# Modulation by quarters: one megabyte holds two feature tiles by 1024 columns, added up in SBUF

## The chip, the core and the metric

One core of a Trainium2 chip runs the whole program once per execution. The metric is the device time of one execution in microseconds. A trace of one profiled execution shows every instruction on the engines: PE (matrix multiply, with its weight loads listed apart as PEld), DVE (vector), ACT (scalar), POOL (GpSimd) and SP, whose queue issues most of the loads.

## The reference

Four transformer layers work on 256 tokens of 1024 features: two layers of a first block (which also carry a context stream of 256 tokens), then a layer with grouped attention and one with a pooling mixer, called the second block here. Each layer first turns a condition vector into six vectors of 1024 (shift, scale and gate, for the mixer and for the feed-forward part):

```python
m = jax.nn.silu(cond) @ w_ada + b_ada                    # 1024 -> 6 * 1024
h = rms_norm(x, gain) * (1 + scale) + shift
x = x + gate * mixer(h);   x = x + gate2 * conv_ffn(...)
```

In the second block the mixer's and the feed-forward part's results are normalised once more before they are added to x. The weights of one modulation are 1024 by 6144 in f32, 24 MB a layer, 96 MB for the four layers. Only two columns (the condition of the tokens and that of the context) are multiplied with them, so each byte is used in one short matmul.

## The kernel before, in words

**Work on PE.** All activations stand feature by token in SBUF. A weight matrix is loaded in pieces of up to 1 MB as two halves `w` (two buffers in all), split by ACT (line 238, `wh`) and DVE (line 240, `wl`) into two parts, and used in three matmuls a tile (`mms`, lines 285, 286, 289). Every third piece puts its split parts into the pool `x8`: seven buffers of 1 MB that also hold `y`, `sx`, `kv`, `qT`, `band` and other whole tensors; some pieces are loaded there whole.

**Modulation units.** A layer's modulation is cut into 24 units; four units make one of the six vectors. `mod_load` (line 362) loads a unit's megabyte, all eight feature tiles by 256 columns, in one piece into `x8` (20 units: those of the opening and the first twelve of layer 1) or as two halves `mw` with three buffers (76 units). `mod_unit` (line 378) issues eight short matmuls (line 387, the trace has two records for each) that leave four partial sums in four groups of 32 partitions, has ACT copy them to SBUF (line 390), calls the load of the following unit, and after a planned wait transposes both halves on PE (line 396), adds the four partial sums up in DVE (line 398) and adds the bias (line 400). `mod_units` makes a list of steps: with `ahead=1` step q loads unit q and computes unit q-1.

**Order.** PE and SP run in the order in which the program is written out, the other engines' orders are made by a planner. Two small programs fix the written order. `spread` mixes the modulation steps evenly into a list of main steps. `Line` holds generators: each yields a cost and a wait, its next part is due after both, and due parts are put in before the next step starts. So a short wait moves a part ahead of steps that follow.

**Second block.** `attention2` projects six chunks, runs eight softmax units (`unit`: scores, line 1178; transposes, line 635; values, line 1198) with twelve modulation units of the last layer (3, 0 to 11) between them, then the output matrix (`wo`), whose results give running sums for the norm (`post_sums`; squares, line 437). Then `post` runs: `post_norm` first sums the squares over features on PE (`rstd`, lines 449, 450), makes the factor `ry` (to line 468), takes two more sums on PE (line 1076), makes `m` (lines 1078 to 1081), a second factor, and the eight `ht` tiles (line 493) that the next matmuls need. `post` mixes four more modulation units in: (3, 12 to 15) after attention, (3, 16 to 19) after the feed-forward part, (3, 20 to 23) after the pooling mixer, where the two sums are ready already (line 1282). The list `late` holds these twelve units. `pool_consts` loads two `band` tiles through `w` after the first post.

The written order of the first post:

```python
def post(self, units, *args):
    self.go(self.post_norm(*args), "p")
    self.run(units)
    self.line.ensure("p")
```

Of the kernel before, what the change touches and what calls it, by code (L numbers as in the profile page):

```python
# [19 lines left out]
P = 128  # L20
D = 1024
NT = 256
# [83 lines left out]
class Stack:  # L106
    def __init__(self, ctx, tc, a, offs, out, upto=None):
# [17 lines left out]
        self.h, self.wm = {}, {}  # L125
# [189 lines left out]
    def setup(self):  # L315
# [16 lines left out]
        self.cpad = [cp.tile([P, KD, 32], F32, name=f"cpad{n}") for n in range(2)]  # L332
        for n in range(2):
            nc.vector.memset(self.cpad[n], 0.0)
            nc.scalar.activation(self.cpad[n][:, :, 0:2], cv[:, n], AF.Silu)
# [26 lines left out]
    def mod_load(self, i, n, x8=True):  # L362
        src = self.a[f"wmod{i}"][n * P * CH:(n + 1) * P * CH].rearrange("(p n) -> p n", p=P)
        if x8:
            w = self.x8("wm")
            self.nc.sync.dma_start(out=w, in_=src)
            w = w.rearrange("p (e k c) -> p e k c", e=2, k=4)
            self.wm[i, n] = [w[:, e] for e in range(2)]
            return
        self.wm[i, n] = [self.mod_half(i, n, e) for e in range(2)]  # L370

    def mod_half(self, i, n, e):
        w = self.mp.tile([P, 4, NT], F32, tag="mw", name="mw", bufs=3)
        src = self.a[f"wmod{i}"][n * P * CH:(n + 1) * P * CH].rearrange("(p n) -> p n", p=P)
        self.nc.sync.dma_start(out=w, in_=src[:, 1024 * e:1024 * e + 1024].rearrange("p (k c) -> p k c", k=4))
        return w

    def mod_unit(self, i, n, then=None):
# [3 lines left out]
        cpad = self.cpad[i // 2]  # L382
        acc = self.psum("acc", [P, 512])[:, :256]
        w = self.wm.pop((i, n))
# [18 lines left out]
    def mod_units(self, i, ns, x8=False, ahead=1):  # L403

        ns = [n if i is None else (i, n) for n in ns]

        def step(q):
            load = (lambda: self.mod_load(*ns[q], x8)) if q < len(ns) else (lambda: None)
            if q >= ahead:
                yield from self.mod_unit(*ns[q - ahead], load)  # L410
# [549 lines left out]
    def ffn(self, i, T, streams, after):  # L960
# [70 lines left out]
        for q in streams:  # L1031
            for ft in range(KD):
                self.go(down(len(groups) - 1, ft, slice(256 * q, 256 * q + 256)))
            after(q, nst[q], y)
# [30 lines left out]
    def post_norm(self, i, y, st, j, g):  # L1065
# [3 lines left out]
        yield 0, 1.2  # L1069
        ry = self.rstd(st)  # L1070
        yield 0.9, 1.5
# [81 lines left out]
    def attention2(self):  # L1153
# [59 lines left out]
        f = self.more_units((3, 0, 12))  # L1213
        seq = kx + vx + q[0] + q[1] + need("c0", "c1", "c2") + f[:2]
        seq += spread(un[0], f[2:5]) + q[2] + need("c3") + spread(un[1], f[5:7]) + q[3] + need("c4")
        seq += spread(un[2], f[7:10]) + need("c5") + spread(un[3], f[10:])
# [17 lines left out]
        for cc in range(4):  # L1234
            for f2 in range(2):
                self.go(wo(cc, f2))
        return y, nst
# [13 lines left out]
    def pool_mixer(self):  # L1251
# [34 lines left out]
        for n in (0, 1, -1, -2, 2, -3, -4, 3, -5, -6, -7, -8):  # L1286
            self.go(z(n) if n >= 0 else out(-n - 1), f"z{n}")
        line.ensure(*(f"z{-n - 1}" for n in range(KD)))
# [288 lines left out]
```

## Time and profile before

| | us |
|---|---|
| Median of 3 runs (lowest, highest) | 1829.44 (1826.78, 1840.67) |
| The profiled execution's own time | 1839.73 |
| Its span, first to last instruction | 1837.9 |
| PE busy | 1650.7 (90%) |
| DVE busy | 1180.2 (64%) |
| ACT busy | 900.9 (49%) |
| POOL busy | 133.0 (7%) |
| Moved by DMA | 288.39 MB, mean 157 GB/s |

The profiled execution's time is the span and 1.8 us around it. Busy shares are averages over stages with different limits; a stage's own rows say which wait ends last there.

### The profile page before, as it was taken

Reading aid. Unit: us, or ns where it says so; the run is one execution under the profiler, and the core shown is the slowest. Engines: PE = TensorE matmul, PEld = TensorE weight load, DVE = VectorE, ACT = ScalarE, POOL = GpSimd, SP = SyncE. Lnnn points to the kernel's source line nnn. Section 1 sums busy time; section 2 is a strip of 40 time slices with the busy share of each in tenths; the row PEclk is TensorE's granted clock in tenths of the full one; section 3 lists DMA queues with packets and bytes.
Section 4 is the critical chain, followed back from the end, with each engine's and each line's share of the span. In section 5 each row is a group of like instructions: output and inputs, shape, how many; then the busy total and the mean of one; then the engine's idle time right before and its main releaser. Section 6 shows DMA issues by size and latency. Waiting matters only on the chain.

```text
span 1837.9 us, 32872 instructions
## 1 busy us (share of the span) xinstructions
PE 1650.7 (90%) x12736; PEld 1443.7 (79%) x12736; DVE 1180.2 (64%) x2992; ACT 900.9 (49%) x2213; POOL 133.0 (7%) x162
## 2 busy tenths in 40 slices
PE   6999797999999998897799999969779999769997
PEld 5877457989889898874488888856659998459997
DVE  5665786656554567865688576746556567666665
ACT  5445554534333334554456464534446565546563
POOL 1000001000000000000001011000221012221010
PEclk9999898999999999997989999989969999789998
DMA  7334330433334332355627767465455544345552
GB/s 310 102 138 152 108 123 24 138 136 117 114 117 138 115 117 70 121 201 184 220 96 280 247 220 246 132 218 172 131 191 173 186 167 155 124 152 188 178 193 84
DMA packets 74892, 288.39 MB, mean 157 GB/s; under 512 B 8560, under 2 KB 9840, under 8 KB 69104
## 3 DMA queue, kind: packets, MB, share of 16 engines
q1 hardware_dynamic: 73152, 283.91, 45.3%
q10 hardware_dynamic: 1584, 2.38, 0.4%
q8 instruction: 100, 1.64, 0.4%
q14 instruction: 56, 0.46, 0.1%
HBM read 285.21 MB, written 1.05 MB: 156 GB/s over the span
## 4 chain that ended last, share of the span: by engine, by line
PE 65%; DVE 13%; DMA 13%; ACT 6%; issue 2%; POOL 1%; SPq 0%; ACTq 0%; DVEq 0%; POOLq 0%
PE S L285 9%; PE S L286 9%; PE S L289 9%; PE acc L285 8%; PE acc L289 8%; PE acc L286 8%; DMA mw<-in_wmod_dram 5%; DVE wl L240 4%; DMA w<-in_wup_dram 4%; PE acc L387 4%; DMA w<-in_wdn_dram 3%; ACT wh L238 2%; DVE ht L493 1%; PE tr L635 1%; PE tr L396 1%
## 5 line engine op out<-in xcount | busy, mean ns | idle before, releaser
L240 DVE TENSOR_TENSOR wl<-w,wh 128x384 fp32r<-128x384 f32 (+2 forms) x1010 | 488.0, 523 | 249.8 <-ACT wh L238 224.4
L238 ACT CAST wh<-w 128x384 fp32r<-128x384 f32 (+2 forms) x1010 | 419.8, 475 | 313.1 <-PE S L286 88.3
L285 PE MATMUL S<-hH,wh 128*128 128x256 f32 x1408 | 350.3, 286 | 20.6 <-ACT hH L503 13.6
L286 PE MATMUL S<-hL,wh 128*128 128x256 f32 x1408 | 348.4, 285 | 4.2 <-POOL hL L501 2.8
L285 PEld LDWEIGHTS S<-hH,wh 128*128 128x128 f32 x1408 | 270.7, 192 | 27.4 <-ACT hH L503 14.4
L286 PEld LDWEIGHTS S<-hL,wh 128*128 128x128 f32 x1408 | 270.5, 192 | 6.5 <-POOL hL L501 3.5
L285 PE MATMUL acc<-gH,wh 128*128 128x256 f32 (+1 forms) x728 | 209.9, 312 | 13.8 <-DVE xc L944 5.5
L286 PE MATMUL acc<-gL,wh 128*128 128x256 f32 (+1 forms) x728 | 205.3, 306 | 0.0
L289 PE MATMUL S<-hH,wl 128*128 128x256 f32 x1408 | 198.3, 284 | 0.0
L289 PEld LDWEIGHTS S<-hH,wl 128*128 128x128 f32 x1408 | 182.5, 193 | 0.0
L285 PEld LDWEIGHTS acc<-gH,wh 128*128 128x128 f32 x728 | 138.8, 191 | 29.3 <-DVE x L944 5.9
L387 PE MATMUL acc<-mw,cpad 128*32 128x256 f32 x1216 | 95.8, 427 | 60.9 <-DMA mw<-in_wmod_dram 60.4
L289 PE MATMUL acc<-gH,wl 128*128 128x256 f32 (+1 forms) x728 | 146.0, 306 | 0.0
L286 PEld LDWEIGHTS acc<-gL,wh 128*128 128x128 f32 x728 | 139.0, 191 | 5.7
L289 PEld LDWEIGHTS acc<-gH,wl 128*128 128x128 f32 x728 | 110.4, 191 | 6.5
L387 PEld LDWEIGHTS acc<-mw,cpad 128*32 128x32 f32 x1216 | 31.6, 115 | 105.9 <-DMA mw<-in_wmod_dram 51.5
L955 DVE SCALAR_TENSOR_TENSOR cgv<-S,sm,cgv 128x255 f32<-128x255 f32 (+1 forms) x132 | 74.9, 568 | 39.5 <-ACT cgv L952 39.1
L285 PE MATMUL acc<-wh,hH 128*128 128x256 f32 x344 | 92.4, 299 | 7.5 <-ACT hH L503 5.5
L390 ACT COPY modsb<-acc 128x256 f32<-128x256 f32 x96 | 35.5, 370 | 127.0 <-PE acc L387 126.3
L952 ACT ACTIVATE cgv<-S,sm 128x256 f32<-128x256 f32 (+1 forms) x132 | 82.8, 627 | 24.8 <-PE S L289 24.8
L993 POOL TENSOR_TENSOR gL<-cgv,gH 128x256 fp32r<-128x256 f32 x66 | 51.7, 783 | 543.6 <-ACT gH L992 525.7
L286 PE MATMUL acc<-wl,hH 128*128 128x256 f32 x344 | 88.6, 288 | 0.0
(261 smaller groups left out, 3011.2 us busy)
## 6 DMA issues: line engine op xcount, KB each, us to landing
mw<-in_wmod_dram SPq DMA_DIRECT2D x152, 512.0 KB, 5.0
w<-in_wup_dram SPq DMA_DIRECT2D x140, 512.0 KB, 4.1
w<-in_wdn_dram SPq DMA_DIRECT2D x56, 512.0 KB, 3.7
wm<-in_wmod_dram SPq DMA_DIRECT2D x20, 1024.0 KB, 7.7
w<-in_wup_dram SPq DMA_DIRECT2D x18, 1024.0 KB, 7.6
w<-in_win_dram SPq DMA_DIRECT2D x32, 512.0 KB, 4.2
w<-in_wout_dram SPq DMA_DIRECT2D x16, 512.0 KB, 5.5
w<-in_wqkv_dram SPq DMA_DIRECT2D x16, 512.0 KB, 4.2
```

The costliest lines, as they stand in the source:

```text
L238: self.nc.scalar.copy(h[:, c:d], w[:, c - a:d - a])
L240: self.nc.vector.tensor_tensor(l[:, c:d], w[:, c - a:d - a], h[:, c:d].bitcast(F32), ALU.subtract)
L285: mm(o, lhsT=s[0], rhs=m[0], start=k == ks[0], stop=False)
L286: mm(o, lhsT=s[0], rhs=m[1], start=False, stop=False)
L289: mm(o, lhsT=S(b, k)[1], rhs=M(b, k)[0], start=False, stop=end and k == ks[-1])
L387: nc.tensor.matmul(acc[32 * q:32 * q + 32], lhsT=cpad[:, k], rhs=w[k // 4][:, q], start=k < 4, stop=k >= 4)
L390: nc.scalar.copy(sb, acc)
L396: nc.tensor.transpose(tr[:, t].rearrange("p q v -> p (q v)"), sb[:, P * t:P * t + P], self.ident)
L493: nc.vector.scalar_tensor_tensor(t, self.xs[s][:, ft], A, r, ALU.mult, ALU.mult)
L952: nc.scalar.activation(out, ps, AF.Identity, scale=cw[:, n + f:n + f + 1], bias=cb[:, f:f + 1])
L955: nc.vector.scalar_tensor_tensor(o[:, :, 1:256], x[:, :, 0:255], cw[:, f:f + 1], o[:, :, 1:256], ALU.mult, ALU.add)
L993: (nc.vector if T == 512 else nc.gpsimd).tensor_tensor(gL[:, a], c[:, 1, :T], gH[:, a].bitcast(F32), ALU.subtract)
```

## The change

- Outside the opening, a unit is now a quarter of a vector's contraction: two feature tiles by all 1024 columns of the vector. `mod_part` issues eight matmuls again (two accumulate in each of four groups), and the sums of four units are added up in SBUF: the first is copied by ACT, the other three are added by DVE from PSUM. Transposes and the bias add come once for four units. The weights in memory are packed to match.
- One zero-padded condition tile holds both blocks' columns.
- The units of attention in the second block are loaded whole into `x8`, two units ahead.
- The twelve late units are three lists of four, loaded into `x8` three ahead: `early_loads` issues the first three loads of each list behind feature tiles 3, 4 and 5 of the work ahead of the post (output matrix, last group of the feed-forward part, pooling mixer); the fourth load is issued in the post.
- `post_norm`'s first two planned waits go from 1.2 and 1.5 to 0.8 each.

```diff
@@ -364,24 +364,21 @@
         if x8:
             w = self.x8("wm")
             self.nc.sync.dma_start(out=w, in_=src)
-            w = w.rearrange("p (e k c) -> p e k c", e=2, k=4)
-            self.wm[i, n] = [w[:, e] for e in range(2)]
+            self.wm[i, n] = [w[:, 1024 * e:1024 * e + 1024] for e in range(2)]
             return
-        self.wm[i, n] = [self.mod_half(i, n, e) for e in range(2)]
-
-    def mod_half(self, i, n, e):
-        w = self.mp.tile([P, 4, NT], F32, tag="mw", name="mw", bufs=3)
-        src = self.a[f"wmod{i}"][n * P * CH:(n + 1) * P * CH].rearrange("(p n) -> p n", p=P)
-        self.nc.sync.dma_start(out=w, in_=src[:, 1024 * e:1024 * e + 1024].rearrange("p (k c) -> p k c", k=4))
-        return w
+        self.wm[i, n] = []
+        for e in range(2):
+            w = self.mp.tile([P, 1024], F32, tag="mw", name="mw", bufs=3)
+            self.nc.sync.dma_start(out=w, in_=src[:, 1024 * e:1024 * e + 1024])
+            self.wm[i, n].append(w)
 
     def mod_unit(self, i, n, then=None):
 
 
         nc = self.nc
-        cpad = self.cpad[i // 2]
+        cpad = self.cpad
         acc = self.psum("acc", [P, 512])[:, :256]
-        w = self.wm.pop((i, n))
+        w = [x.rearrange("p (k c) -> p k c", k=4) for x in self.wm.pop((i, n))]
         for k in range(KD):
             q = k % 4
             nc.tensor.matmul(acc[32 * q:32 * q + 32], lhsT=cpad[:, k], rhs=w[k // 4][:, q], start=k < 4,
@@ -400,14 +397,43 @@
         nc.vector.tensor_tensor(m, m, b.unsqueeze(2).to_broadcast([P, 2, 2]), ALU.add)
         yield 0.22, 0
 
-    def mod_units(self, i, ns, x8=False, ahead=1):
-
-        ns = [n if i is None else (i, n) for n in ns]
+    def mod_part(self, i, n, then=None):
+
+
+        nc = self.nc
+        j, q = divmod(n, 4)
+        cpad = self.cpad
+        acc = self.psum("acc", [P, 512])[:, :256]
+        w = self.wm.pop((i, n))
+        for e in range(2):
+            for u in range(4):
+                nc.tensor.matmul(acc[32 * u:32 * u + 32], lhsT=cpad[:, 2 * q + e], rhs=w[e][:, 256 * u:256 * u + 256],
+                                 start=e == 0, stop=e == 1)
+        if q == 0:
+            self.msum[i, j] = self.mp.tile([P, NT], F32, tag="msum", name="msum", bufs=1)
+            nc.scalar.copy(self.msum[i, j], acc)
+        else:
+            nc.vector.tensor_tensor(self.msum[i, j], self.msum[i, j], acc, ALU.add)
+        if then is not None:
+            then()
+        yield 0.9, WAIT["mod"] if q == 3 else 0
+        if q < 3:
+            return
+        sb = self.msum.pop((i, j))
+        tr = self.psum("tr", [P, 2, 4, 32])
+        for t in range(2):
+            nc.tensor.transpose(tr[:, t].rearrange("p u v -> p (u v)"), sb[:, P * t:P * t + P], self.ident)
+        b = self.sm(f"sm{i}", "b")[:, KD * j:KD * j + KD].rearrange("p (u t) -> p t u", t=2)
+        nc.vector.tensor_tensor(self.mod[i][:, j].rearrange("p (u t) v -> p t u v", t=2), tr[:, :, :, i // 2 * 2:i // 2 * 2 + 2],
+                                b.unsqueeze(3).to_broadcast([P, 2, 4, 2]), ALU.add)
+        yield 0.22, 0
+
+    def mod_units(self, ns, x8=False, ahead=1):
 
         def step(q):
             load = (lambda: self.mod_load(*ns[q], x8)) if q < len(ns) else (lambda: None)
             if q >= ahead:
-                yield from self.mod_unit(*ns[q - ahead], load)
+                yield from self.mod_part(*ns[q - ahead], load)
             else:
                 load()
 
@@ -1031,6 +1057,8 @@
         for q in streams:
             for ft in range(KD):
                 self.go(down(len(groups) - 1, ft, slice(256 * q, 256 * q + 256)))
+                if i == 2:
+                    self.early_loads(ft)
             after(q, nst[q], y)
 
 
@@ -1066,9 +1094,9 @@
 
 
         nc = self.nc
-        yield 0, 1.2
+        yield 0, 0.8
         ry = self.rstd(st)
-        yield 0.9, 1.5
+        yield 0.9, 0.8
         ps = st.get("S")
         if ps is None:
             ps = self.psum("S", [P, 2, 512])
@@ -1210,10 +1238,10 @@
         kx, vx = chunk(0, lambda acc, s: self.post_k(acc, s, tk)), chunk(1, self.post_v)
         q = [chunk(2 + c, post_q(c)) for c in range(4)]
         un = units()
-        f = self.more_units((3, 0, 12))
-        seq = kx + vx + q[0] + q[1] + need("c0", "c1", "c2") + f[:2]
-        seq += spread(un[0], f[2:5]) + q[2] + need("c3") + spread(un[1], f[5:7]) + q[3] + need("c4")
-        seq += spread(un[2], f[7:10]) + need("c5") + spread(un[3], f[10:])
+        f = self.more_units((3, 0, 12), x8=True, ahead=2)
+        seq = f[:1] + kx + vx + f[1:2] + q[0] + q[1] + need("c0", "c1", "c2")
+        seq += spread(un[0], f[2:5]) + q[2] + need("c3") + spread(un[1], f[5:8]) + q[3] + need("c4")
+        seq += spread(un[2], f[8:11]) + need("c5") + spread(un[3], f[11:])
         seq += need(*(f"a{hp}1" for hp in range(4)))
         for u in seq:
             u()
@@ -1234,6 +1262,7 @@
         for cc in range(4):
             for f2 in range(2):
                 self.go(wo(cc, f2))
+                self.early_loads(2 * cc + f2)
         return y, nst
 
     def pool_consts(self):
@@ -1285,6 +1314,8 @@
         nst["S"] = self.psum("S", [P, 2, 512])
         for n in (0, 1, -1, -2, 2, -3, -4, 3, -5, -6, -7, -8):
             self.go(z(n) if n >= 0 else out(-n - 1), f"z{n}")
+            if n < 0:
+                self.early_loads(-n - 1)
         line.ensure(*(f"z{-n - 1}" for n in range(KD)))
         return y, nst
 
@@ -1293,22 +1324,28 @@
 
         if l:
             return [], []
-        u = self.mod_units(0, range(8, 24))
+        u = self.more_units((0, 8, 24))
         return u[:12], u[12:]
 
     def fill_f(self, i):
 
         if i == 0:
-            return self.mod_units(1, range(0, 12), True)
+            return self.more_units((1, 0, 12), x8=True)
         return self.more_units((2, 8, 24)) if i == 1 else []
 
-    def more_units(self, *parts):
-        return self.mod_units(None, [(i, n) for i, a, b in parts for n in range(a, b)])
-
-    def post(self, units, *args):
-
+    def more_units(self, *parts, **kw):
+        return self.mod_units([(i, n) for i, a, b in parts for n in range(a, b)], **kw)
+
+    def early_loads(self, ft):
+
+        if 3 <= ft < 6 and self.late:
+            self.late[0][ft - 3]()
+
+    def post(self, *args):
+
+        units = self.late.pop(0)
         self.go(self.post_norm(*args), "p")
-        self.run(units)
+        self.run(units[3:])
         self.line.ensure("p")
 
     def run(self, units):
@@ -1403,19 +1440,19 @@
         if self.upto == "L1":
             return self.finish()
 
-        self.late = self.more_units((3, 12, 24))
+        self.late = [self.more_units((3, n, n + 4), x8=True, ahead=3) for n in (12, 16, 20)]
         y, st = self.attention2()
-        self.post(self.late[:5], 2, y, st, 3, self.sm("sm2", "n2g"))
+        self.post(2, y, st, 3, self.sm("sm2", "n2g"))
         self.pool_consts()
 
         def after2(q, st, y):
-            self.post(self.late[5:9], 3, y, st, 0, self.sm("sm3", "n1g"))
+            self.post(3, y, st, 0, self.sm("sm3", "n1g"))
 
         self.ffn(2, 256, (0,), after2)
         if self.upto == "S0":
             return self.finish()
         y, st = self.pool_mixer()
-        self.post(self.late[9:], 3, y, st, 3, self.sm("sm3", "n2g"))
+        self.post(3, y, st, 3, self.sm("sm3", "n2g"))
 
         def after3(q, st, y):
             self.go(self.post_last(y, st), "p")
@@ -1514,8 +1551,10 @@
             parts.append(kchunk(w, full, c))
         return chunks(parts)
 
-    def packed_mod(w):
-        return chunks([kchunk(w, full, slice(256 * n, 256 * n + 256)) for n in range(24)])
+    def packed_mod(w, first=0):
+        return chunks([kchunk(w, full, slice(256 * n, 256 * n + 256)) for n in range(first)]
+                      + [kchunk(w, (2 * q, 2 * q + 1), slice(1024 * j, 1024 * j + 1024))
+                         for j in range(first // 4, 6) for q in range(4)])
 
     for l in range(2):
         w = g["w_in"][l][:, order]
@@ -1525,7 +1564,7 @@
                                 for q in range(2) for c in range(2)])
         a[f"wup{l}"] = packed_up(g["w_up"][l])
         a[f"wdn{l}"] = packed_down(g["w_down"][l], 512 if l == 0 else 256)
-        a[f"wmod{l}"] = packed_mod(g["w_ada"][l])
+        a[f"wmod{l}"] = packed_mod(g["w_ada"][l], 8 if l == 0 else 0)
         a[f"ws{l}"] = cat(g["a_ws"][l].transpose(2, 0, 1))
         smalls(f"sm{l}", [
             ("b", cols(g["b_ada"][l])), ("n1g", cols(g["norm1_g"][l])), ("n2g", cols(g["norm2_g"][l])),
```

## Rows read from the trace of the kernel before

**Rows 1.** The chain that ended last, from the page: by engine, then by line.

```profile
PE 65%; DVE 13%; DMA 13%; ACT 6%; issue 2%; POOL 1%; SPq 0%; ACTq 0%; DVEq 0%; POOLq 0%
PE S L285 9%; PE S L286 9%; PE S L289 9%; PE acc L285 8%; PE acc L289 8%; PE acc L286 8%; DMA mw<-in_wmod_dram 5%; DVE wl L240 4%; DMA w<-in_wup_dram 4%; PE acc L387 4%; DMA w<-in_wdn_dram 3%; ACT wh L238 2%; DVE ht L493 1%; PE tr L635 1%; PE tr L396 1%
```

**Rows 2.** The same chain in order of time: start, length, what was waited for.

```profile
1209.03 8.44 DMA mw<-in_wmod_dram
...
1292.42 4.64 DMA mw<-in_wmod_dram
...
1325.27 8.08 DMA mw<-in_wmod_dram
...
1607.54 4.30 DMA mw<-in_wmod_dram
...
1616.99 7.72 DMA w<-in_wup_dram
```

**Rows 3.** Waits on SP's queue, whole span: total, times, longest.

```profile
SPq L375 <- PE acc L387: 393.5, 87, 27.5
```

**Rows 4.** PE's waits from 1177 to 1305 us, longest first.

```profile
PE acc L387 <- DMA mw<-in_wmod_dram: 21.7, 6, 9.4
```

**Rows 5.** Stretches: PE, PEld, DVE, ACT, POOL busy, granted clock, DMA share, GB/s.

```profile
1177.00:1300.00 123.00, 95.43 (x672) 70.46 (x671) 69.78 (x197) 52.52 (x134) 3.56 (x4) 0.90 0.51 171
1300.00:1328.00 28.00, 27.61 (x210) 26.62 (x208) 19.61 (x46) 15.15 (x38) 8.84 (x11) 0.97 0.32 104
```

**Rows 6.** Costliest groups on the page: the modulation matmuls.

```profile
L387 PE MATMUL acc<-mw,cpad 128*32 128x256 f32 x1216 | 95.8, 427 | 60.9 <-DMA mw<-in_wmod_dram 60.4
```

**Rows 7.** Line 396 alone in a stretch: PE, PEld, clock, DMA, GB/s.

```profile
330.00:700.00 370.00, 4.20 (x22) 2.98 (x22) 1.00 0.37 123
```

**Rows 8.** Single lines: duration min/median/max in ns.

```profile
L390 ACT COPY modsb<-acc x96: 352/372/396, 19.2 to 1620.9; 128x256 f32<-128x256 f32 x96
...
L398 DVE TENSOR_REDUCE mod<-tr x96: 152/174/176, 21.1 to 1622.3; 128x4 f32<-128x16 f32 x96
...
L1015 DVE TENSOR_TENSOR y<-y,acc x32: 407/417/423, 1519.7 to 1824.7; 128x256 f32<-128x256 f32 x32
```

**Rows 9.** Timeline of the first post (start, length, engine, line, operation).

```profile
1329.93 0.41 ACT L437 ACTIVATE sq<-y 128x256 f32<-128x256 f32 x1
...
1339.67 1.22 PE L449 MATMUL tr<-nacc,ones 128*128 128x256 f32 x2
...
1344.24 0.43 DVE L468 SCALAR_TENSOR_TENSOR rstd<-var,rstd 128x256 f32<-128x256 f32 x1
...
1351.13 0.42 DVE L1078 TENSOR_TENSOR m<-S,rstd 128x256 f32<-128x256 f32 x1 [6.46 <-PE S L1076]
...
1356.76 0.58 PE L285 MATMUL S<-hH,wh 128*128 128x256 f32 x1 [4.82 <-ACT hH L503]
```

**Rows 10.** Timeline of the second post.

```profile
1560.75 0.41 ACT L437 ACTIVATE sq<-y 128x256 f32<-128x256 f32 x1
...
1568.30 1.22 PE L449 MATMUL tr<-nacc,ones 128*128 128x256 f32 x2
...
1579.43 0.42 DVE L1078 TENSOR_TENSOR m<-S,rstd 128x256 f32<-128x256 f32 x1 [6.14 <-PE S L1076]
```

**Rows 11.** Timeline of the third post.

```profile
1606.21 0.70 PE L1282 MATMUL S<-yy,ones 128*128 128x256 f32 x2
...
1612.44 1.16 PE L449 MATMUL tr<-nacc,ones 128*128 128x256 f32 x2
...
1621.36 0.41 DVE L1079 SCALAR_TENSOR_TENSOR m<-S,m 128x256 f32<-128x256 f32 x1
...
1628.79 1.27 DVE L493 SCALAR_TENSOR_TENSOR ht<-x,mscale,rstd 128x256 f32<-128x256 f32 x3
```

**Rows 12.** Loads on the page: count, KB each, median us to landing.

```profile
mw<-in_wmod_dram SPq DMA_DIRECT2D x152, 512.0 KB, 5.0
...
wm<-in_wmod_dram SPq DMA_DIRECT2D x20, 1024.0 KB, 7.7
```

More of the change, by code (lines that the diff above doesn't have):

```diff
@@ L124, in __init__ @@
         self.evac_n = 0
-        self.h, self.wm = {}, {}
+        self.h, self.wm, self.msum = {}, {}, {}
         self.done = {}
@@ L331, in setup @@
         nc.vector.memset(self.eps, EPS)
-        self.cpad = [cp.tile([P, KD, 32], F32, name=f"cpad{n}") for n in range(2)]
+        self.cpad = cp.tile([P, KD, 32], F32, name="cpad")
+        nc.vector.memset(self.cpad, 0.0)
         for n in range(2):
-            nc.vector.memset(self.cpad[n], 0.0)
-            nc.scalar.activation(self.cpad[n][:, :, 0:2], cv[:, n], AF.Silu)
+            nc.scalar.activation(self.cpad[:, :, 2 * n:2 * n + 2], cv[:, n], AF.Silu)
         self.lnexp()
```

## The prediction

> **What bounds the kernel now.** I read the chain of waits first. PE carries 65% of it and DMA 13% [rows 1], so the kernel is a PE kernel with holes, and a change must fill holes or take away PE work that stands in full stretches. One hole belongs to modulation: the waits for `mw`, 5% of the chain, some 94 us. In order of time these waits lie in three places. Five stand in the second block's attention, from 1209.03 to 1292.42 us, 27.1 us together; six stand in the three posts, from 1325.27 to 1607.54 us, 32.6 us together, and one wait for `w` of 7.72 us follows the last of them [rows 2]. The rest, some 34 us, lies in stages whose loads the change leaves as they are.
>
> Why the loads come late is seen on SP: its `mw` loads waited 393.5 us for matmuls to free one of three half buffers [rows 3]. A load starts when the matmul before it ends, so PE pays its landing. PE's own waits say the same: in the attention 21.7 us in six waits, the longest 9.4 [rows 4], in a stretch of 123 us where PE is busy for 95.4 us at a granted clock of 0.90 and DVE for 69.8, with DMA busy half the time [rows 5].
>
> **Part 1: fewer transposes and copies.** There are 96 units, eight of them in the opening, which keep their form. Of the other 88, three in four (66) lose two transposes, a copy and two small DVE operations. The matmuls stay eight a unit, 1.26 us (95.8 us over 76 units) [rows 6]; the merged condition tile and the packing cost nothing, the streams are as long as before. Two transposes take 0.38 us (4.20 us for 22) in the first feed-forward part, where the clock is 1.00 [rows 7]. Nine units lose them there: 3.4 us, counted whole. In the first attention and in the second feed-forward part twelve each lose 4.6 us; there PE has holes of its own and I count half, 4.6 us for both. In the second layer's attention fifteen lose them, but its units stay behind loads that do not change: 0. Together 8 us (bounds: 3.4 alone; 18 if all 48 count).
>
> On ACT 66 copies of 0.372 us go, 24.6 us. On DVE 66 adds of 0.417 us come (the nearest row is an add of the same shape from PSUM) and 66 reductions of 0.174 us go [rows 8]: at most +16 us on an engine that is 64% busy, less by the bias adds that go too. What hides it is DVE's idle third. Without that cover the price is at most 3 us in the second feed-forward part (12 x 0.243), where DVE's splits are on the chain, and ACT's 12 copies in front of the same splits (4.5 us) pay it back. I take 0.
>
> **Part 2: the three posts.** PE runs in written order, so the sums of squares (line 449) stand behind two units that wait for loads. In the first post the last square is ready at 1330.34 but line 449 starts at 1339.67: 9.3 us lost. From there `ry` takes 5.0 us, to 1344.67; `m` could start then, but starts at 1351.13, since line 1076 stands behind two more units: 6.0 us more with the handover taken off. From `m` to the first matmul it is 5.6 us, which stays [rows 9]. With the loads landed, unit 12 fits before the squares are ready, and the shorter planned waits put line 1076 behind unit 13 instead of unit 15. Gain 15.3 us. Late next are the casts of the next weights: the last square stands behind a cast on ACT that waits for `w`, and the early loads go in front of that `w` on SP. I take 14 (bounds 10 and 15.3).
>
> In the second post the square is ready at 1561.2 and line 449 starts at 1568.30 (7.1 us); from there to `m` it is 11.1 us [rows 10] against 5.0 in the first, so 6.1 more. Here DVE's splits may hold `ry` back by a microsecond: 12 (bounds 9 and 13.2).
>
> In the third the pooling's last sums end at 1606.9; a unit of 1.1 to 1.3 us would let line 449 start near 1608 instead of 1612.44: 4.4 us. `m`'s second step stands behind a reduction of a late unit and comes at 1621.36; the `ht` tiles begin at 1628.79 [rows 11], 16.4 us after line 449. With its gap closed, the first post's way from line 449 to the first matmul, which lies behind `ht`, is 5.0 + 5.6 = 10.6 us. So at least 5.8 us more can go, 10.2 in all. Three adds of the new form (1.3 us) stand among DVE's steps of the norm, and the first splits too: I take 8.5 (bounds 4.4 and 10.2). The wait of 7.72 us for `w` is under these steps, not added: SP reaches that load once it no longer stands behind `mw`.
>
> Posts together 34.5 us (bounds 23 and 39).
>
> **Part 3: the second block's attention.** Twelve loads move forward past the loads of `wqkv` and `wo` on SP. Three waiting units at most are live; with `kv`, `sx` and `qT` that is six of seven buffers, so none should wait for room. The 21.7 us of PE's waits [rows 4] go, and nine units' transposes, 3.4 us. Late next is softmax: scores no longer wait 9.4 us for a unit in front of them, and PE can reach a transpose before DVE and ACT have made it. DVE's 69.8 us in 123 [rows 5] leave room for the same work in 100. I take 18.5 of 25 (bounds 8 and 25).
>
> **Part 4: what the early loads cost.** Nine loads of 1 MB move into stages that load weights. The stage of `wo`, 1300 to 1328 us, moves 104 GB/s with DMA busy 0.32 [rows 5]; three megabytes more in 28 us are 112 GB/s, and the attention already moves 171. Within that cover they cost nothing on PE, at worst the landing of a megabyte where a weight half stands behind it. A megabyte lands 7.7 us after its issue, a half 5.0 [rows 12]. The fourth load of a post is issued some 3 units ahead of its use, and only the two sums of line 1076, which stand in front of it, are on the path.
>
> [...]
>
> **The sum.** 8 + 34.5 + 18.5 = 61 us, which takes the profiled execution from 1839.7 to 1779. It is 10 us above the median of the runs, so the forecast is 1829.4 - 61 = 1768 us.
>
> **The rivals.**
>
> *The waits only move.* Softmax and the weights' casts take over where the loads stop. For it: DVE is at 57% in the attention and the last square stands behind a cast. Against it: the posts' gaps stand between operations whose inputs were ready. Then only half of the posts, 5 us of the attention and the transposes remain: 17 + 5 + 8 = 30, 1799 us.
>
> *SP stalls for room.* `x8` has seven buffers; a modulation load that finds none blocks everything behind it on SP, and the `w` halves have two buffers only, so PE starves. Each such stall costs about a landing, 7.7 us [rows 12]. The places are the `wo` stage (`sx`, `y`, a weight pair and three units are seven with the next) and the last group of the feed-forward part (`sx`, `y`, `band`, a pair, two units, and the third waits). It decides from 8 stalls on (61 / 7.7); with all twelve late loads it costs 92 us: 1829 + 92 - 61 = 1860 us, slower. Against it: the room opens when the pair's matmuls end, a few microseconds later, and the weights behind are two pieces ahead.
>
> *The change does not load ahead.* If the planner's buffers let the loads go only when they went before, only the transposes are won: 1821 us. SP's row speaks against it: the loads waited for half buffers, which the change does not use there.
>
> *More than the sum.* If the transposes count whole and every gap closes, 18 + 39 + 25 = 82: 1747 us.
>
> **How the numbers follow.** Forecast 0.60 (own range 1752 to 1788), the waits only move 0.20, the slower rival 0.06, no loading ahead 0.08, more than the sum 0.06. The range of 1742 to 1800 takes in the forecast with its bounds, the first rival and the last, and leaves out 0.14 and some tails. A change of 1% is 18 us and about what a measurement tells from none: below 1811 is faster, above 1848 slower. So faster 0.86, within 1% 0.08, slower 0.06.
>
> **What would show it.** Right: no wait for `mw` on PE after 1177 us; line 449 within 2 us of the last square in each post and `m` some 5.5 us behind it; the attention 15 to 20 us shorter; line 396 down from 192 records to 60; the first feed-forward part 3 us shorter. Wrong: waits of SP for room in `x8` with PE waiting for `wl` behind them, ACT casts waiting for `w` in front of the last square, or PE idle in the attention on DVE where it was idle on DMA. Most of all the sum would fall if the feed-forward parts behind the posts start sooner but end no sooner, because their weights set their end.

## The result, and the profile after

The changed kernel takes 1778.2 us, the median of 4 runs (1772.81 to 1784.91), against 1833.18 us for 4 runs of the kernel before: ratio 0.97, 95% interval 0.9644 to 0.9757, so 55 us less. The forecast was 1768, its range 1742 to 1800. The profiled execution took 1774.65 us with a span of 1772.9; that is 65 us less than the profiled execution of before, which was itself 7 to 10 us above the medians of its kernel. A later run of the same changed kernel gave 1777.05 us and a ratio of 0.9694 (0.9672 to 0.9715).

The chain that ended last, on the page after, by engine and by line (answers to [rows 1]):

```profile
PE 63%; DVE 17%; DMA 10%; ACT 6%; issue 3%; POOL 1%; SPq 0%; ACTq 0%; DVEq 0%; POOLq 0%
PE S L285 9%; PE S L286 9%; PE S L289 9%; PE acc L285 8%; PE acc L286 8%; PE acc L289 8%; DVE wl L240 5%; DMA w<-in_wup_dram 4%; PE acc L410 3%; DMA w<-in_wdn_dram 2%; ACT wh L238 2%; PE tr L661 2%; DVE ht L519 1%; DVE mx L651 1%; DMA mw<-in_wmod_dram 1%
```

`mw` has gone from 5% to 1%, DMA as a whole from 13% to 10%, and DVE has risen from 13% to 17%. A small part of that rise is the step of the forecast that failed, below.

PE's waits in the second block's attention after, longest first (answers to [rows 4]):

```profile
PE tr L610 <- DVE mixL L268: 2.7, 2, 2.5
PE S L1206 <- DVE qT L261: 2.5, 1, 2.5
PE acc L285 <- ACT hH L529: 2.3, 1, 2.3
```

No wait for a modulation load is among them; before, there were six with 21.7 us. The same two stages in stretches after (columns as in [rows 5]):

```profile
1167.00:1270.00 103.00, 92.40 (x674) 70.86 (x673) 75.14 (x200) 52.16 (x132) 3.55 (x4) 0.95 0.61 217
1270.00:1293.00 23.00, 23.00 (x197) 22.87 (x199) 15.76 (x34) 13.02 (x32) 8.51 (x11) 1.00 0.61 221
```

The stretch of before in [rows 5] ends 4.4 us ahead of its stage's end. The whole stage, from the norm's sum to the first matmul of the output matrix, before and then after:

```profile
1172.19:1304.38 132.19, 104.62 (x727) 78.76 (x725) 77.30 (x217) 57.49 (x147) 3.56 (x4) 0.90 0.51 168
```

```profile
1162.38:1269.70 107.32, 96.72 (x708) 74.87 (x707) 77.57 (x205) 55.65 (x140) 3.55 (x4) 0.95 0.61 215
```

PE is idle for 10.6 us instead of 27.6 and busy for 96.7 instead of 104.6, and its granted clock is 0.95 instead of 0.90. The stage of the output matrix moves 221 GB/s instead of 104, and PE is still busy in all of it.

SP's waits after, from 1162 to 1570 us:

```profile
SPq L224 <- DVE wl L240: 251.1, 66, 20.0
SPq L366 <- PE acc L410: 36.6, 6, 13.4
...
SPq L366 <- DVE pn L1138: 10.3, 1, 10.3
...
SPq L366 <- PE acc L289: 2.7, 2, 2.3
```

The modulation loads into `x8` (line 366) did stall for room, nine times in this stretch: six times in the attention, 36.6 us in all and up to 13.4 (the row with line 410), and three times with the late units' loads, 13 us. Next to nothing of it reaches PE: from 1162 to 1570 us its only wait for these loads is one of 0.6 us, and it has none for `wl`.

The timeline of the first post after (answers to [rows 9]), and then from `m` to the feed-forward part's first matmul:

```profile
1292.87 1.07 PE L410 MATMUL acc<-wm,cpad 128*32 128x256 f32 x16
...
1293.87 0.70 PE L475 MATMUL tr<-nacc,ones 128*128 128x256 f32 x2
1294.38 0.41 ACT L463 ACTIVATE sq<-y 128x256 f32<-128x256 f32 x1
...
1296.47 1.20 PE L1104 MATMUL S<-sx,ones 128*128 128x256 f32 x4
...
1299.40 0.41 DVE L494 SCALAR_TENSOR_TENSOR rstd<-var,rstd 128x256 f32<-128x256 f32 x1
...
1299.94 1.41 POOL L1135 TENSOR_TENSOR pn<-y,rstd 128x256 f32<-128x256 f32 x2 [3.02 <-PE acc L410]
1300.07 0.41 DVE L1106 TENSOR_TENSOR m<-S,rstd 128x256 f32<-128x256 f32 x1
...
1300.73 0.41 DVE L1107 SCALAR_TENSOR_TENSOR m<-S,m 128x256 f32<-128x256 f32 x1
...
1301.31 1.59 POOL L1136 TENSOR_TENSOR x<-x,pn 128x256 f32<-128x256 f32 x2
...
1301.42 0.90 DVE L1108 TENSOR_TENSOR m<-m,rstd 128x256 f32<-128x256 f32 x1
...
1302.36 0.83 DVE L1109 TENSOR_TENSOR sx<-sx,m 128x256 f32<-128x256 f32 x1
...
1303.11 0.94 DVE L1138 SCALAR_TENSOR_TENSOR pn<-y,G,rstd 128x256 f32<-128x256 f32 x1
...
1303.97 0.82 DVE L490 TENSOR_SCALAR var<-sx 128x256 f32<-128x256 f32 x1
...
1304.59 1.64 POOL L1136 TENSOR_TENSOR x<-x,pn 128x256 f32<-128x256 f32 x2
1304.71 0.94 DVE L1139 TENSOR_TENSOR x<-x,pn 128x256 f32<-128x256 f32 x1
1305.58 0.94 DVE L492 SCALAR_TENSOR_TENSOR var<-var,rstd 128x256 f32<-128x256 f32 x1
...
1306.20 0.90 POOL L1135 TENSOR_TENSOR pn<-y,rstd 128x256 f32<-128x256 f32 x1
1306.55 0.83 DVE L493 TENSOR_TENSOR var<-var,rstd 128x256 f32<-128x256 f32 x1
...
1307.18 0.79 POOL L1136 TENSOR_TENSOR x<-x,pn 128x256 f32<-128x256 f32 x1
1307.42 0.83 DVE L494 SCALAR_TENSOR_TENSOR rstd<-var,rstd 128x256 f32<-128x256 f32 x1
...
1308.57 1.26 DVE L519 SCALAR_TENSOR_TENSOR ht<-x,mscale,rstd 128x256 f32<-128x256 f32 x3
...
1309.63 0.58 PE L285 MATMUL S<-hH,wh 128*128 128x256 f32 x1 [8.34 <-ACT hH L529]
```

The lower half is what to read. From `m` (1300.07) to the first matmul (1309.63) it is 9.6 us; before it was 5.6, with DVE's same steps at 0.42 us. The first post of the kernel before, its last update on POOL and two of DVE's steps:

```profile
1351.07 0.72 POOL L1108 TENSOR_TENSOR x<-x,pn 128x256 f32<-128x256 f32 x1
...
1352.13 0.42 DVE L1080 TENSOR_TENSOR m<-m,rstd 128x256 f32<-128x256 f32 x1
...
1352.58 0.42 DVE L1081 TENSOR_TENSOR sx<-sx,m 128x256 f32<-128x256 f32 x1
```

There POOL began its updates of `x` at 1344.80 and ended the last at 1351.79, in the time that DVE waited for line 1076. After, the sums come early, so POOL's updates and DVE's steps fall into the same time, and until POOL's last update ends every 128x256 DVE step with its operands in SBUF takes 0.82 to 0.94 us. `m`'s first two steps, which read a PSUM bank, stay at 0.41 although both run beside POOL.

Stage lengths in us, each taken from the starts and ends of PE's matmuls in the timelines. Attention: from its norm's sum (line 475; 449 before) to the first matmul of the output matrix. Post: from the last matmul of the stage ahead (in the third, the pooling's last sums) to the first matmul of the feed-forward part; after the slash, the part of it from `m`.

| kernel | attention | post 1 | post 2 | post 3 |
|---|---|---|---|---|
| before | 132.2 | 29.2 / 5.6 | 25.8 / 5.6 | 23.0 / 12.5 |
| changed | 107.3 | 16.7 / 9.6 | 17.4 / 10.4 | 14.6 / 9.6 |
| changed, run again (e9) | 110.9 | 17.7 / 9.6 | 17.4 / 10.4 | 14.6 / 9.6 |
| e1 packing alone | 136.3 | 29.7 / 5.6 | 25.7 / 5.6 | 20.0 / 9.2 |
| e2 attention as before | 133.7 | 17.8 / 9.6 | 17.4 / 10.4 | 14.6 / 9.7 |
| e3 late units as before | 109.9 | 28.7 / 5.6 | 26.1 / 5.6 | 19.9 / 9.3 |
| e4 without POOL's updates | 110.6 | 14.5 / 7.1 | 13.4 / 6.3 | 11.6 / 6.7 |
| e5 waits as before | 112.1 | 18.0 / 9.3 | 17.3 / 8.8 | 15.4 / 9.6 |
| e6 without the late adds | 108.7 | 17.2 / 9.5 | 16.7 / 9.5 | 14.2 / 9.6 |
| e7 chain of `m` in PSUM | 110.6 | 16.3 / 8.7 | 15.7 / 8.6 | 12.7 / 7.7 |
| e8 all updates on DVE | 109.5 | 15.8 / 8.1 | 12.5 / 6.3 | 10.9 / 6.0 |
| e10 first three blocks' units old | 108.4 | 16.8 / 9.6 | 17.4 / 10.4 | 14.6 / 9.7 |
| e11 e7 and tile 0 ahead | 110.1 | 16.3 / 8.4 | 15.7 / 7.9 | 12.7 / 7.4 |

### The profile page after: what moved, and what is told of

Its sections match the earlier page's. It is cut to its first block, busy times and chain, and to the rows that moved or that the text cites. A ratio compares the mean times of both kernels' runs of the same rounds, so it can differ in the third digit from the quotient of the medians.

```text
span 1772.9 us, 32420 instructions
## 1 busy us (share of the span) xinstructions
PE 1618.3 (91%) x12604; PEld 1427.0 (80%) x12604; DVE 1195.8 (67%) x2903; ACT 878.9 (50%) x2147; POOL 135.2 (8%) x162
## 4 chain that ended last, share of the span: by engine, by line
PE 63%; DVE 17%; DMA 10%; ACT 6%; issue 3%; POOL 1%; SPq 0%; ACTq 0%; DVEq 0%; POOLq 0%
PE S L285 9%; PE S L286 9%; PE S L289 9%; PE acc L285 8%; PE acc L286 8%; PE acc L289 8%; DVE wl L240 5%; DMA w<-in_wup_dram 4%; PE acc L410 3%; DMA w<-in_wdn_dram 2%; ACT wh L238 2%; PE tr L661 2%; DVE ht L519 1%; DVE mx L651 1%; DMA mw<-in_wmod_dram 1%
## 5 line engine op out<-in xcount | busy, mean ns | idle before, releaser
L285 PE MATMUL S<-hH,wh 128*128 128x256 f32 x1408 | 352.0, 287 | 25.7 <-ACT hH L529 17.4
L978 ACT ACTIVATE cgv<-S,sm 128x256 f32<-128x256 f32 (+1 forms) x132 | 82.9, 628 | 27.6 <-PE S L289 27.6
L970 DVE SCALAR_TENSOR_TENSOR x<-acc,mod,x 128x256 f32<-128x256 f32 x104 | 50.1, 481 | 61.1 <-PE acc L289 60.7
L286 PE MATMUL S<-hcL,wh 128*128 128x256 f32 x352 | 86.5, 284 | 0.3 <-DVE hcL L530 0.3
L285 PE MATMUL S<-hcH,wh 128*128 128x256 f32 x352 | 86.4, 281 | 0.0
```

The source lines that it names most:

```text
L285: mm(o, lhsT=s[0], rhs=m[0], start=k == ks[0], stop=False)
L286: mm(o, lhsT=s[0], rhs=m[1], start=False, stop=False)
L970: self.nc.vector.scalar_tensor_tensor(x, acc[:, c], self.mods(i, j)[:, ft, s:s + 1], x, ALU.mult, ALU.add)
L978: nc.scalar.activation(out, ps, AF.Identity, scale=cw[:, n + f:n + f + 1], bias=cb[:, f:f + 1])
```

## The experiments

Each ratio is against the kernel before on the same chip; the changed kernel's, for comparison, is 0.9694. A difference of 0.001 in the ratio is 1.8 us.

**e1, e2, e3: one part alone, or one part undone.** e1 keeps the packing and `mod_part`, and gives the attention, the late lists and the planned waits their old form:

```diff
-        f = self.more_units((3, 0, 12), x8=True, ahead=2)
-        seq = f[:1] + kx + vx + f[1:2] + q[0] + q[1] + need("c0", "c1", "c2")
+        f = self.more_units((3, 0, 12))
+        seq = kx + vx + q[0] + q[1] + need("c0", "c1", "c2") + f[:2]
...
-        self.run(units[3:])
+        self.run(units)
...
-        self.late = [self.more_units((3, n, n + 4), x8=True, ahead=3) for n in (12, 16, 20)]
+        late = self.more_units((3, 12, 24))
+        self.late = [late[:5], late[5:9], late[9:]]
```

> Undoes the loads ahead and the two planned waits, keeps the units by quarters and the sums in SBUF. If the gain is made of three nearly independent parts, this keeps only the transposes: 8 to 10 us below the kernel before (ratio about 0.995), with the second block's attention and its three posts as long as before. Rival: the repacking itself matters more (fewer copies on ACT, fewer waits on PE's transposes), then 20 us or more below.

Measured: 1831.41 us, ratio 1.0002 (0.998 to 1.0025): nothing gained, against what was expected. Its attention waited for loads about as long as before, and was 4 us longer. PE's waits there, and the attention as a stretch:

```profile
PE acc L410 <- DMA mw<-in_wmod_dram: 20.2, 8, 9.9
```

```profile
1167.00:1298.00 131.00, 101.78 (x671) 73.96 (x670) 75.74 (x200) 52.01 (x131) 3.56 (x4) 0.86 0.51 171
```

e2 undoes the attention's part of that diff alone in the changed kernel; e3 undoes the late lists and the waits alone.

> The changed kernel with the second block's attention loading its units as before, as halves one unit ahead. Theory: the attention alone is worth 25 us (the waits of 21.7 us and 3.4 us of transposes, less the latter here), so 20 to 24 us above the changed kernel, and PE waits for mw again between the output of the projections and the output matrix. Rival: the attention becomes bound by softmax as well, then 10 us or less above.

Measured: 1800.74 us, ratio 0.9838 (0.9799 to 0.9878), so 26 us above the changed kernel by the ratios; the attention took 133.7 us, with 17.4 us of PE's waits on `mw`. That is as expected within the interval. The waits are not the whole of it, though; the stage in e2:

```profile
1164.18:1297.90 133.72, 106.92 (x709) 78.79 (x707) 78.32 (x205) 55.51 (x140) 3.56 (x4) 0.86 0.54 179
```

Against the changed kernel's stage PE is idle for 16.2 us more, and with the same instructions (709 records against 708) it is also busy for 10.2 us more, at a granted clock of 0.86 instead of 0.95.

> The changed kernel with the twelve late units loaded in the posts as before and the planned waits 1.2 and 1.5. Theory: the three posts are worth 29 us, so 27 to 31 us above the changed kernel, each post 8 to 13 us longer from its last matmul to the next, and DVE's steps behind m back at 0.42 us in the first two posts, since POOL is done by then. Rival: part of the gain comes from the loads moved out of SP's way for the weights behind; then the feed-forward parts get longer too and the sum is above 35 us.

Measured: 1804.98 us, ratio 0.9865 (0.9823 to 0.9907), 31 us above the changed kernel by the ratios, the upper end of what was expected. The norm's matmul comes 10.4, 8.3 and 6.1 us after the stage's last matmul again, instead of 0.93, and in posts 1 and 2 `m` to the first matmul is back to 5.6 us: POOL was done at 1315.8 when `m` started at 1316.77. So the longer chain behind `m` belongs to the early start of `m`.

**e4, e6, e7, e8: what makes the way behind `m` longer.** e4 drops POOL's two lines in `post_x`, so it leaves out the update of x for five tiles in each post; e6 leaves out the adds of the late units:

```diff
-            nc.gpsimd.tensor_tensor(t, y[:, ft], ry, ALU.mult)
-            nc.gpsimd.tensor_tensor(x, x, t, ALU.add)
+            pass
```

> The changed kernel, which leaves out POOL's ten small operations in each of the three posts (the update of x for feature tiles 1 to 5). Theory, POOL beside DVE: DVE's steps from m to the first ht tile take 0.42 us again instead of 0.8 to 0.95, so from m to the first matmul 5.6 to 6.5 us instead of 9.6 to 10.4 and the kernel is 9 to 12 us below the changed one. Rival, the adds of the late units and the weight splits in DVE's queue: the steps stay at 0.8 to 0.95 us and the time changes by less than 3 us.

Measured: 1769.9 us, ratio 0.9666 (0.9628 to 0.9704): 5 us below the changed kernel by the ratios, with an interval of 7 on either side; the posts' stages lost 9.2 us together. The step lines of `m` show it directly. Lines 1107 to 1109 in the changed kernel, then 1108 and 1109 in e4 (min/median/max ns over the three posts):

```profile
L1107 DVE SCALAR_TENSOR_TENSOR m<-S,m x3: 407/411/418, 1300.7 to 1554.8; 128x256 f32<-128x256 f32 x3
...
L1108 DVE TENSOR_TENSOR m<-m,rstd x3: 430/897/965, 1301.4 to 1555.5; 128x256 f32<-128x256 f32 x3
...
L1109 DVE TENSOR_TENSOR sx<-sx,m x3: 412/827/941, 1302.4 to 1556.4; 128x256 f32<-128x256 f32 x3
```

```profile
L1108 DVE TENSOR_TENSOR m<-m,rstd x3: 410/412/415, 1305.9 to 1552.2; 128x256 f32<-128x256 f32 x3
...
L1109 DVE TENSOR_TENSOR sx<-sx,m x3: 410/425/425, 1306.4 to 1552.7; 128x256 f32<-128x256 f32 x3
```

Without POOL's updates the same steps take 0.41 us. The cause is confirmed. The 9.2 us of the stages lie in the 9 to 12 us expected; the 5 us of the whole are less, but are not told apart from them. `m` to the first matmul stays 0.7 to 1.5 us over the 5.6 of before.

```diff
-        else:
+        elif not (i == 3 and n >= 12):
             nc.vector.tensor_tensor(self.msum[i, j], self.msum[i, j], acc, ALU.add)
```

> The changed kernel, which leaves out DVE's three adds of partial sums for each of the three late vectors, nine in all. Theory, POOL beside DVE: m to first matmul shortens by at most two adds, 0.8 us a post; 1 to 3 us below the changed kernel, and the steps stay at 0.8 to 0.95 us. Rival, the adds in DVE's queue are what lengthens the step: 3 to 4 us a post, 9 to 12 us below.

Measured: 1772.93 us, ratio 0.9674 (0.9656 to 0.9692), not told apart from the changed kernel's 0.9694. `m` to the first matmul stays at 9.5, 9.5 and 9.6 us, so the adds among DVE's steps are not the cause.

e7 leaves POOL as it is and moves `m` and the variance into the unused half of the PSUM bank of the sums:

```diff
+        mp, vp = ps[:, 0, NT:], ps[:, 1, NT:]
-        nc.vector.scalar_tensor_tensor(m, ps[:, 0, :NT], 2.0, m, ALU.mult, ALU.add)
-        nc.vector.tensor_tensor(m, m, ry, ALU.mult)
-        im = nc.vector.tensor_tensor(sx, sx, m, ALU.add)
+        nc.vector.scalar_tensor_tensor(mp, ps[:, 0, :NT], 2.0, m, ALU.mult, ALU.add)
+        nc.vector.tensor_tensor(mp, mp, ry, ALU.mult)
+        im = nc.vector.tensor_tensor(mp, sx, mp, ALU.add)
...
-        rx = self.rstd_of(sx)
+        rx = self.tp.tile([P, NT], F32, tag="rstd", name="rstd")
+        self.rsqrt(rx, vp, mp, 1.0 / D)
+        if (i, j) != (3, 3):
+            nc.scalar.copy(sx, mp)
```

> The changed kernel with m and the variance of post_norm kept in the free half of the sums' PSUM banks, so that each of DVE's six steps from m's third on has one operand in PSUM; one ACT copy more a post. Theory: steps with an operand in PSUM are not slowed beside POOL (the adds from PSUM take 0.40 us there), so six steps lose 0.4 us each: 2 to 3 us a post, 6 to 9 us below the changed kernel. Rival, every DVE operation is slowed beside POOL or the operands don't matter: within 2 us of the changed kernel.

Measured: 1774.22 us, ratio 0.9676 (0.9655 to 0.9696). The posts' stages are 4 us shorter, less than expected, and the whole is not told apart from the changed kernel's 0.9694. The first post of e7, DVE's steps with POOL beside them:

```profile
1308.72 0.42 DVE L1109 TENSOR_TENSOR S<-S,rstd 128x256 f32<-128x256 f32 x1
...
1309.18 0.43 DVE L1110 TENSOR_TENSOR S<-sx,S 128x256 f32<-128x256 f32 x1
1309.52 0.78 DVE L1142 SCALAR_TENSOR_TENSOR pn<-y,G,rstd 128x256 f32<-128x256 f32 x1
...
1310.34 0.83 DVE L1143 TENSOR_TENSOR x<-x,pn 128x256 f32<-128x256 f32 x1
...
1311.09 0.42 DVE L490 TENSOR_SCALAR S<-S 128x256 f32<-128x256 f32 x1
...
1312.46 0.43 DVE L492 SCALAR_TENSOR_TENSOR S<-S,rstd 128x256 f32<-128x256 f32 x1 [0.95 <-ACT rstd L491]
```

Steps with one operand in PSUM take 0.42 us beside POOL; the two that update tile 0, all in SBUF, still take 0.78 and 0.83. So the mechanism is confirmed; what is left of the longer way is tile 0's two steps and, in this post, the wait of 0.95 us for ACT's exponential at line 492.

e8 gives all updates of `x` in the posts to DVE:

```diff
-        return {"G": G, "pool": (6, 7) if i == 3 and j == 5 else POOL_X}
+        return {"G": G, "pool": (6, 7) if i == 3 and j == 5 else ()}
```

> The changed kernel with the update of x for all eight feature tiles on DVE and none on POOL. Theory: DVE's steps take 0.42 us again, m to first matmul falls to about 6 us, but five more pairs of 0.9 us stand among the h tiles, 4.5 us a post, partly under PE's first matmuls: between 6 us below and 3 us above the changed kernel. Rival, no slowing by POOL: 8 to 13 us above.

Measured: 1786.04 us, ratio 0.9736 (0.9708 to 0.9765), 8 us slower than the changed kernel by the ratios, though the two intervals overlap a little. That is in the rival's range and outside the theory's; yet the theory's mechanism is in the trace, where lines 1108 and 1109 take 0.42 us again and the posts became 9.5 us shorter in all. What it had mis-sized is the price of the updates on DVE: from the first post's norm sum to the second's it took 223.7 us, against 217.0 in the changed kernel, as they come back between the `ht` tiles. POOL's help seems worth more than the contention costs.

**e5: the planned waits.** The changed kernel with `post_norm`'s waits of before:

```diff
-        yield 0, 0.8
+        yield 0, 1.2
...
-        yield 0.9, 0.8
+        yield 0.9, 1.5
```

> The changed kernel with post_norm's planned waits of 1.2 and 1.5 as before. Theory: with the loads landed the order matters by the length of one or two units only: line 1104's sums move behind two more units, m comes 1 to 2 us later in the first two posts, so 2 to 4 us above the changed kernel. Rival: the waits carry the posts' gain, then 10 us or more above.

Measured: 1777.21 us, ratio 0.9695 (0.9671 to 0.9718). The norm's matmul came 1.8 to 1.9 us after the last matmul and not 0.93, and the three posts were 2 us longer together, but the time is the same. That is under the 2 to 4 us expected and far from the rival's 10: the wait change carries nothing that these runs can tell.

**e9, e10, e11: part 1 from the other side, and one more version.**

> The changed kernel once more, for a second profile and as the neighbour on the same chip of the two kernels below. Expected: 1774 to 1782 us, ratio 0.968 to 0.972; its posts 16 to 18, 16.5 to 18 and 14 to 16 us from last to next matmul, so that stages which differ by more than that between two kernels differ by their code.

e9 is the changed kernel again; measured 1777.05 us, ratio 0.9694 (0.9672 to 0.9715). Its posts differ from those of its first profile by up to 1.0 us and its attention by 3.6, which bounds what one profile of a stage can say.

```diff
-                yield from self.mod_part(*ns[q - ahead], load)
+                part = self.mod_part if ns[q - ahead][0] == 3 else self.mod_unit
+                yield from part(*ns[q - ahead], load)
```

> The changed kernel, with the first three blocks' modulation units back in their old form (two transposes, a copy and a reduction in each); the fourth block's units, their packing and their early loads stay. Theory from the packing alone (ratio 1.0002): the transposes were worth nothing that is seen in the end, since PE finds as much room elsewhere or gets a lower clock for it: 1774 to 1782 us, within 3 us of the changed kernel, and the third feed-forward part's start (the attention's norm) within 4 us of the changed kernel's 1162. The prediction's part 1 (8 us, bounds 3.4 to 18): 1782 to 1796 us, and that norm 8 to 10 us later, near 1172.

Measured: 1783.29 us, ratio 0.9734 (0.9714 to 0.9755), 0.004 above e9, which is 7 us with an uncertainty of about 5. That is on the prediction's side, against what e1 had made me expect. The expectation's other sign does not decide: the attention's norm came at 1166.4 us, between the 1162 of the theory and the 1172 of the prediction's side, and in the eleven profiles with the new units up to there it lies anywhere from 1157.4 to 1167.7. One stage does tell the two forms apart: in the first feed-forward part, from the second norm's sum to the third's, it took 391.0 us in e10 and 390.9 before, but 389.2 or 389.3 in all eleven others. Where the rest of the 7 us lies is not shown.

e11 is e7 with tile 0's update moved ahead of `m`:

```diff
         ry = self.rstd(st)
+        self.post_x(y, ry, st, 0)
         yield 0.9, 0.8
...
-        with self.tc.issue_after(im.ins):
-            self.post_x(y, ry, st, 0)
```

> The changed kernel with the chain from m to the stream's variance in the unused half of the PSUM bank, and tile 0's update of x on VectorE ahead of m and no longer between m and the variance. Theory (VectorE's steps between SBUF operands are lengthened by GpSimd's, and the two steps of tile 0 stand in the chain): m to first matmul 6.5 to 8 us, 1768 to 1774 us, 5 to 9 below the changed kernel. Rival (the first tile ahead of m delays m by what it saves behind it, and the feed-forward part is held by its weights): 1773 to 1779 us.

Measured: 1774.09 us, ratio 0.9676 (0.9655 to 0.9698). Beside the changed kernel on the same chip (1777.05) that is 3 us, just outside the theory's range and inside the rival's, and the intervals overlap. The way from `m` fell to 8.4, 7.9 and 7.4 us, but `m` itself came 0.4 to 0.8 us later than in e7, as the rival had it: as a whole e11's posts are as long as e7's. Both versions are faster than the kernel before; that they beat the changed kernel is not shown.

## Why the prediction was right, and where it was not

**The bound and the likeliest case held.** The loads came late because they stood behind one another for half buffers, and with them early PE's waits on them went. Undone one at a time, the attention is worth 26 us, the late units 31 and the first blocks' packing 7. These sum to 64 against a whole of 56; the excess is within their intervals (7 and 8 us on the first two). That the sum of 61 us came so near is in part luck: part 2 fell short by 5 us and part 3 went over by 6, each for a reason that the forecast did not hold.

**Part 1, forecast 8 us.** e10 gives 7; e1 gives 0 (an interval of 4 on either side). Both can stand: in e1 the attention still waits for its loads and came out 4 us longer, at a granted clock of 0.86 where it was 0.90 before [rows 5]. PE is busy for 107.0 us of its stage against 104.6 before, with fewer transposes; that the lower clock is the reason is an argument from one profile of each, not shown. So part 1 lies somewhere from 0 to 7 us, and the one stage that tells, the first feed-forward part, gave 1.7 us where 3.4 was counted. Line 425 leaves 44 records against 192 on line 396; the 16 in the opening complete the 60 that were foretold.

**Part 2, forecast 34.5 us; the stages show 29.3.** The first step was right and a little low. The norm's matmul now follows the last matmul by 0.93 us in each post, which wins 11.1, 8.1 and 4.6 us where 9.3, 7.1 and 4.4 were counted. From there to `m` it is 6.2 and 6.1 us in posts 1 and 2, close to the foretold 5.5. **The step that failed is "From `m` to the first matmul it is 5.6 us, which stays".** It became 9.6 and 10.4 us, 3.9 and 4.7 longer, and 9.6 in the third post, where the 10.6 us counted from line 449 on had 5.6 in them. The 5.6 was measured in a post whose `m` came 6.5 us late [rows 9], and that delay had hidden POOL's seven microseconds of updates. Take the delay away and the two engines meet. e4 (POOL's work out), e7 (PSUM operands) and e3 (`m` late again) each bring back the short steps, in three different ways; e6 rules out the added sums. The profile of before held the warning: in its third post one step of line 1080 took 0.935 us where the other two took 0.416, since POOL was running there (to 1624.6):

```profile
L1080 DVE TENSOR_TENSOR m<-m,rstd x3: 415/416/935, 1352.1 to 1622.4; 128x256 f32<-128x256 f32 x3
```

The prediction read that post's late second step off its place behind a reduction, and did not look at the steps' own lengths.

**Part 3, forecast 18.5 us of 25.** The profile shows 24.9, e9 21.3, e2 26 by the ratios: nearer the upper bound, but not by the way that was counted. The discount was for PE waiting on softmax next, and in part that came: in the whole stage PE's idle time other than on modulation loads rose from 5.9 us (27.6 less 21.7) to 10.6, all of it on DVE and ACT. What the sum had put at nothing is PE's busy time beyond the transposes: it fell by 7.9 us where 3.4 were counted, and by 10.2 between e2 and the changed kernel, which have the same instructions there. Also wrong is "none should wait for room": six of the attention's loads did, 36.6 us on SP, without a wait on PE.

**Part 4, forecast 0.** Held. The output matrix's stage takes 23.2 us before and after, at twice the bytes a second; the feed-forward part behind the second block's first post takes 200.3 us from its first to its last matmul (202.5 before), and the one behind the third post 195.8 to its norm's sum (194.7). A megabyte lands in 7.6 us (7.7 before).

**The rivals.** "SP stalls for room" was right that stalls come and wrong that they reach PE: nine in the stretch, one above the eight from which it was to decide, and 0.6 us of waiting on PE. Six of them came in the attention, where it had named no place. The count was the wrong test: a stall on SP cost PE no landing here, since the weights behind were far enough ahead that PE had no wait for `wl`. "The waits only move" has a true core, at a smaller price: new limits did take the place of the waits, 8.6 us in two posts and 4.7 in the attention, but in the posts it was DVE beside POOL, not the casts.

## What to carry to other kernels

When a wait is taken out of a chain, the steps behind it do not keep their lengths: look at which engine used the wait to do work of its own, and price the steps as they run beside that work. A step's length in another place of the same trace, where the engines overlap, is the better row. A load that waits for a half-size buffer is best moved to a place where a stall costs no one, and a stall on the load queue is harmless as long as what stands behind it is early.

## What the runs showed of the hardware

**VectorE beside GpSimd.** For 128x256 f32 a DVE step with two operands in SBUF takes 0.41 to 0.48 us alone and mostly 0.82 to 0.97 us while POOL works on SBUF tensors; with an operand in PSUM it takes 0.41 to 0.43 us either way. A step with a single SBUF operand (line 490) takes 0.28 us alone before and 0.82 beside POOL, and 0.42 with PSUM. POOL pays too: its updates went from a median of 0.726 us to 0.899. POOL's multiplication, before and after:

```profile
L1107 POOL TENSOR_TENSOR pn<-y,rstd x15: 720/726/909, 1344.8 to 1623.0; 128x256 f32<-128x256 f32 x15
```

```profile
L1135 POOL TENSOR_TENSOR pn<-y,rstd x15: 722/899/1042, 1299.9 to 1560.7; 128x256 f32<-128x256 f32 x15
```

The two engines take turns. In the timeline of the first post after, line 1109 ends at 1303.19 behind POOL's pair that ends at 1302.90, line 492 at 1306.52 behind 1306.23, line 493 at 1307.38 behind 1307.10, line 494 at 1308.25 behind 1307.97. In all three posts of that trace every lengthened two-operand step of the list ends 0.28 to 0.29 us after the POOL update beside which it began (line 490 0.15), and every POOL update that began beside such a step ends 0.58 to 0.59 us after it. One turn of each is 0.86 to 0.88 us, which is where the some 0.9 us of both come from.

The Trainium skill's page "SBUF — State Buffer", section "Who interferes with whom", says that a DVE instruction with two SBUF inputs contends with a GpSimd instruction that reads SBUF, and one with at most one SBUF input, outside the two-port modes, does not. The runs agree: e7's steps are the second kind, and line 490 is a `tensor_scalar`, which the page counts among those that can enter a two-port mode. The page calls the shared ports an exclusive lock, and says of the two-port modes that the later instruction blocks fully. The ends above agree with a lock, for two SBUF inputs too: neither engine runs at half speed beside the other, each waits for the other's turn.

**The clock of a stage with load waits.** The attention ran at a granted clock of 0.90 before and at 0.95 after, with PE's waits on loads gone: between the two levels of 1.2 and 2.4 GHz the stage spends less time at the lower one. What that gives back can be read where the instructions are the same. With the old loads PE is busy for 106.9 us in e2 and 107.0 in e1, at 0.86; with the units loaded ahead it is busy for 96.1 to 99.4 us in ten profiles, at 0.94 to 0.97. So taking out the waits also shortened the work between them by some 8 to 11 us.
